# 128-row products in the scores and the compressed branch, and the softmax scaled on ScalarE with reciprocals taken a pack at a time

## The chip, the cores and the metric

One core of one Trainium2 chip runs the whole program. The metric is the device time of one execution in microseconds. TensorE (PE) does the matrix products and the transposes, VectorE (DVE) and ScalarE (ACT) the element-wise work, GpSimd (POOL) more of it, and SyncE (SP) issues every DMA. Each engine has its own queue of instructions.

## What is computed

Two decoder layers over 512 tokens of width 1024, in float32. One projection of the normed input feeds four groups of 4 heads x 64 wide: A (dilated windows), B (latent attention), C (compressed, selected and sliding-window attention, gated) and D (stick-breaking, no softmax). Each group's output is gated, then one output projection, a norm and the residual follow. Cut to what matters here:

```python
# A, B and the two block branches of C: per head and 128-query block
s = q @ k.T * scale                     # causal or dilated mask
p = exp(s - max(s)); p = p / sum(p)     # softmax
o = p @ v                               # C: times sigmoid(gate) per query
# C, compressed: 31 compressed keys/values of 64, all 4 heads
p_cmp = softmax(mask(q @ kc.T)); o_cmp = p_cmp @ vc
# D: z = q @ k.T * d**-0.5, then log-space products, a @ v
# layer: x + rms_norm(concat(o * silu(g)) @ w_out, g_post)
```

## The kernel before

Float32 operands are split into a high and a low part (type fp32r) and multiplied in three products, high x high, high x low and low x high; the fourth is dropped. All tiles of the two arenas (`arena_r` for split operands, `arena_f` for float32) are 512 columns wide. Of PSUM's eight banks, two hold scores, two hold transposes, one the outputs, and three take the projections.

The program is written as two generators per layer. `main` runs attention D, then B, C and A. `fill` runs the projections, gates and compressions, and last the output projection. `mix` (L1395 on) interleaves them by the ratios in `RATIO`. A scheduler then lays the instructions of each engine out in an order found by a model of the time at build, with the attention's instructions at raised priority. On the chip each engine runs its list in that order.

Attention goes by packs: one score bank of up to 512 columns holds one to four segments, and a segment is one head (in C one branch and head) and one query block `i`, 128*(i+1) columns wide. In one layer B has 10 packs, C 22 and A 11, together 64 segments; over both layers 86 packs and 128 segments. For A, C and D a score segment takes two products (`scores`, L973 and L974): stacked queries hold the high part in rows 0 to 63 and the low part in rows 64 to 127, the stacked keys hold the high part twice, so L973 does two of the three products with 128 rows, and L974 adds high query x low key with 64 rows. `scores_pair` (L983) does the same for two short segments of C. B keeps its own form (L964 to L966, 96 rows, three products).

`softmax` then goes segment by segment: a masked row extreme on DVE (L1016) gives the bias, ACT takes the exponential and its sum (L1018), DVE takes the reciprocal (L1019), in C multiplies it by the gate (L1022), and scales the segment (L1023). `turn` transposes 128x128 blocks on PE (L1100), splits them on ACT (L1103) and DVE (L1104), and `pv` multiplies with the values (L1116).

The compressed branch keeps its keys in one tile (`kcmp`, made at L936 to L940) and its scores in `cmp_soft` (L1066 with 128 rows, L1067 with 64, four heads). Its values (`vcmp`, L945 to L948) sit in rows 32h to 32h+31 for head h, and `pv` is called on 32 rows at a time.

Keys of A and C are put together by `key_stack` (DMAs within SBUF, all at L530), keys of D by `d_key` (L798 the high part, L801 the low part, one DMA for the copy of the high part). `split` makes the weights' high part on ACT or DVE (L307, L313, L315) and the low part on POOL (L308, L318) as weights come in (L282).

## Time and profile before

| | |
|---|---|
| median of three runs | 745.35 us (745.24 to 746.9) |
| profiled execution | 745.8 us, its span 744.0 us |
| TensorE clock granted, mean of the span | 0.959 |
| PE / DVE / ACT / POOL busy | 691.3 / 558.5 / 424.5 / 393.4 us |
| products and transposes on PE | 3464 |

Busy time is the union of an engine's instructions, and a product's end is modelled: consecutive products overlap in the records, so the time from one product's start to the next one's start tells what PE spends on it. Weight loads (PEld) stand on a row of their own and overlap the products. In the views below, a line that begins with a stretch such as 150.00:340.00 tells the busy time and the count of each engine in it; "idle ... <-" tells what ended an engine's idle time.

In time, layer 0 has D's scores from 56 to about 109 us, B from 150, C from 205 and A from 293 to 340 us; layer 1 has D from 410 to 466, B from 507, C from 563 and A from 650 to 700 us. Projections fill PE between and during these.

### The profile page before, as it was taken

Reading aid. Unit: us, or ns where it says so; the run is one execution under the profiler, and the core shown is the slowest. Engines: PE = TensorE matmul, PEld = TensorE weight load, DVE = VectorE, ACT = ScalarE, POOL = GpSimd, SP = SyncE. Lnnn points to the kernel's source line nnn. Section 1 sums busy time; section 2 is a strip of 40 time slices with the busy share of each in tenths; the row PEclk is TensorE's granted clock in tenths of the full one; section 3 lists DMA queues with packets and bytes.
Section 4 is the critical chain, followed back from the end, with each engine's and each line's share of the span. In section 5 each row is a group of like instructions: output and inputs, shape, how many; then the busy total and the mean of one; then the engine's idle time right before and its main releaser. Section 6 shows DMA issues by size and latency. Waiting matters only on the chain.

```text
span 744.0 us, 10331 instructions
## 1 busy us (share of the span) xinstructions
PE 691.3 (93%) x3464; PEld 544.7 (73%) x3464; DVE 558.5 (75%) x1150; ACT 424.5 (57%) x917; POOL 393.4 (53%) x299
## 2 busy tenths in 40 slices
PE   7998899399999999999979999979899998999996
PEld 6986677287866778768869787757786775877785
DVE  4937989879779698677693666987868889766833
ACT  5335676376467445785442666848745644566822
POOL 3828326665875242594581244286658526247710
PEclk9999899699998999999999999989999999899999
DMA  8437211634163024443442231047425204321041
GB/s 314 141 80 226 63 33 31 139 93 134 40 188 106 13 81 114 152 147 116 146 172 79 61 96 42 1 76 207 119 66 156 86 0 142 85 83 60 29 142 57
DMA packets 33733, 76.61 MB, mean 103 GB/s; under 512 B 6736, under 2 KB 15312, under 8 KB 33680
## 3 DMA queue, kind: packets, MB, share of 16 engines
q1 hardware_dynamic: 33680, 75.95, 33.8%
q8 instruction: 27, 0.44, 0.2%
q14 instruction: 26, 0.21, 0.1%
HBM read 57.71 MB, written 4.19 MB: 83 GB/s over the span
## 4 chain that ended last, share of the span: by engine, by line
PE 55%; DVE 27%; ACT 5%; issue 5%; SPq 3%; DMA 3%; POOL 2%; DVEq 0%; ACTq 0%; POOLq 0%
PE bank L454 8%; PE bank L455 7%; PE bank L457 6%; PE bank L446 5%; PE bank L444 5%; PE bank L445 5%; PE bank L1116 5%; PE bank L1100 4%; PE bank L974 4%; DVE arena_f L1052 3%; SPq L530 2%; PE bank L973 2%; DVE stats L1022 2%; DVE arena_f L1023 2%; DVE arena_f L873 2%
## 5 line engine op out<-in xcount | busy, mean ns | idle before, releaser
L318 POOL TENSOR_TENSOR arena_r<-raw,arena_r 128x512 fp32r<-128x512 f32 (+1 forms) x150 | 209.1, 1415 | 158.8 <-ACT arena_r L313 92.0
L454 PE MATMUL bank<-arena_r 128*128 128x512 f32 (+1 forms) x416 | 166.2, 404 | 21.2 <-DVE arena_r L780 17.8
L455 PE MATMUL bank<-arena_r 128*128 128x512 f32 (+1 forms) x416 | 163.7, 398 | 2.6 <-DVE arena_r L430 2.6
L454 PEld LDWEIGHTS bank<-arena_r 128*128 128x128 f32 x416 | 83.5, 201 | 39.8 <-DVE arena_r L780 18.5
L457 PE MATMUL bank<-arena_r 128*128 128x512 f32 (+1 forms) x416 | 108.8, 387 | 0.0
L444 PE MATMUL bank<-arena_r 128*128 128x256 f32 (+1 forms) x280 | 97.1, 347 | 1.5 <-ACT arena_r L429 1.4
L455 PEld LDWEIGHTS bank<-arena_r 128*128 128x128 f32 x416 | 83.7, 201 | 18.7 <-DVE arena_r L430 3.0
L445 PE MATMUL bank<-arena_r 128*128 128x256 f32 (+1 forms) x280 | 97.0, 346 | 0.0
L1018 ACT ACTIVATE arena_f<-arena_f,stats 128x384 f32<-128x384 f32 (+3 forms) x128 | 71.3, 559 | 43.9 <-DVE stats L1016 43.5
L446 PE MATMUL bank<-arena_r 128*128 128x256 f32 (+1 forms) x280 | 95.1, 346 | 0.0
L1104 DVE TENSOR_TENSOR arena_r<-bank,arena_r 128x512 fp32r<-128x512 f32 (+2 forms) x122 | 71.7, 597 | 30.7 <-ACT arena_r L1103 29.8
L1116 PE MATMUL bank<-arena_r 128*128 128x256 f32 (+5 forms) x368 | 84.0, 323 | 5.2 <-DVE arena_r L1104 4.2
L457 PEld LDWEIGHTS bank<-arena_r 128*128 128x128 f32 x416 | 73.7, 193 | 14.8 <-issue 2.1
L1103 ACT CAST arena_r<-bank 128x512 fp32r<-128x512 f32 (+2 forms) x122 | 61.1, 514 | 35.2 <-PE bank L1100 32.6
L1100 PE MATMUL bank<-consts,arena_f 128*128 128x128 f32 x408 | 74.8, 282 | 3.5 <-DVE arena_r L1104 3.4
L1016 DVE CUSTOM_DVE_ANT_0 arena_f<-bank,consts 128x512 f32<-128x512 f32 (+3 forms) x128 | 58.7, 483 | 20.9 <-PE bank L974 14.0
L1023 DVE TENSOR_SCALAR arena_f<-arena_f,stats 128x384 f32<-128x384 f32 (+3 forms) x128 | 72.9, 585 | 1.9
L308 POOL TENSOR_TENSOR arena_r<-raw,arena_r 128x512 fp32r<-128x512 f32 x34 | 47.7, 1414 | 46.3 <-ACT arena_r L307 37.1
L313 ACT CAST arena_r<-raw 128x1024 fp32r<-128x1024 f32 (+2 forms) x55 | 56.1, 1024 | 27.0 <-DMA raw<-w_in 10.9
L1116 PEld LDWEIGHTS bank<-arena_r 128*128 128x128 f32 (+2 forms) x368 | 51.7, 163 | 18.6 <-DVE arena_r L1104 5.3
L1100 PEld LDWEIGHTS bank<-consts,arena_f 128*128 128x128 f32 x408 | 52.2, 144 | 17.6 <-DVE arena_r L1104 5.1
L444 PEld LDWEIGHTS bank<-arena_r 128*128 128x128 f32 x280 | 53.9, 193 | 8.4 <-ACT arena_r L429 1.6
(163 smaller groups left out, 1226.4 us busy)
## 6 DMA issues: line engine op xcount, KB each, us to landing
raw<-w_in SPq DMA_DIRECT2D x56, 512.0 KB, 3.9
raw<-w_out SPq DMA_DIRECT2D x16, 512.0 KB, 3.3
arena_r<-arena_r SPq DMA_DIRECT2D x104, 64.0 KB, 2.0
arena_f<-x SPq DMA_DIRECT2D x8, 512.0 KB, 3.8
raw<-w1k SPq DMA_DIRECT2D x8, 512.0 KB, 3.8
arena_r<-arena_r SPq DMA_DIRECT2D x32, 128.0 KB, 2.5
raw<-w1v SPq DMA_DIRECT2D x8, 512.0 KB, 3.9
arena_f<-xs SPq DMA_DIRECT2D x4, 512.0 KB, 3.6
```

The lines of the kernel that those rows point to most:

```text
L318: nc.gpsimd.tensor_tensor(lo[:, q], raw[:, q], h[:, q].bitcast(F32), OP.subtract)
L444: mm(out, wh, xh, start=start, stop=False, skip_group_check=True)
L445: mm(out, wh, xl, start=False, stop=False, skip_group_check=True)
L446: mm(out, wl, xh, start=False, stop=stop, skip_group_check=True)
L454: mm(out[:, q], wh[:, k, :], self.h(0, k)[:, q], start=k == 0, stop=False, skip_group_check=True)
L455: mm(out[:, q], wh[:, k, :], self.h(1, k)[:, q], start=False, stop=False, skip_group_check=True)
L457: mm(out[:, q], wl[:, k - 8, :], self.h(0, k - 8)[:, q], start=False, stop=k == 15, skip_group_check=True)
L1018: nc.scalar.activation(x, x, AF.Exp, bias=nm, scale=-1.0, accum_out=l)
L1023: nc.vector.tensor_scalar(x, x, r, None, op0=OP.mult)
L1100: nc.tensor.transpose(t[:, 128 * j:128 * j + 128], b, self.ident)
L1104: nc.vector.tensor_tensor(lo[:, :w], t[:, :w], hi[:, :w].bitcast(F32), OP.subtract)
L1116: mm(o, v, x, start=first and n == 0, stop=last and n == 2 * len(jobs) - 1, skip_group_check=True)
```

## The change

Two parts.

Rows. Every low product of the scores (L974, L983, L1067) gets the full 128 rows. For that the low part of the keys is put twice into the stack, by wider DMAs in `key_stack` and by one more DMA in `d_key`; the product now also adds low x low. The compressed values go into a zeroed tile, head h in columns 128h to 128h+127 and rows 32h to 32h+31, so that `pv` can use all 128 rows for each head.

Softmax. The exponentials of a whole pack are taken first, then one reciprocal for the pack, then each segment is scaled by an ACT copy with the reciprocal as its scale. In C the gate is still multiplied in per segment on DVE.

```diff
@@ key_stack
-            self.dma(s[64 + 32 * j:96 + 32 * j, 0:512], p[:, 0:512])
+            self.dma(s[64 + 32 * j:96 + 32 * j], p)
@@ d_key, after the two subtractions of L801
+            self.dma(b[64:128], b[0:64])
@@ compress, keys
-            nc.vector.tensor_tensor(s[0:64, 352:384], o2[0:64, 0:32], s[0:64, 96:128].bitcast(F32), OP.subtract)
+            nc.vector.tensor_tensor(s[:, 352:384], o2[:, 0:32], s[:, 96:128].bitcast(F32), OP.subtract)
@@ compress, values
-            nc.scalar.copy(s[:, 0:64], o2[:, 0:64])
-            nc.vector.tensor_tensor(s[:, 64:128], o2[:, 0:64], s[:, 0:64].bitcast(F32), OP.subtract)
+            nc.vector.memset(s.ap.bitcast(F32), 0.0)
+            for h in range(4):
+                r, c = slice(32 * h, 32 * h + 32), 128 * h
+                nc.scalar.copy(s[r, c:c + 64], o2[r, 0:64])
+                nc.vector.tensor_tensor(s[r, c + 64:c + 128], o2[r, 0:64], s[r, c:c + 64].bitcast(F32), OP.subtract)
@@ scores
-        mm(out, qs[0:64, q], kb[0:64, :n], start=False, stop=True, skip_group_check=True)
+        mm(out, qs[:, q], kb[:, :n], start=False, stop=True, skip_group_check=True)
@@ scores_pair: x = k[0:r, ...] and Cq[h][0:r, ...] with r = 128, 64 become k[:, ...] and Cq[h][:, ...]
...
@@ softmax
-        a = 0
-        for br, h, i in segs:
+        a, k = 0, len(segs)
+        nm, l, r = self.col(k), self.col(k), self.col(k)
+        parts = []
+        for j, (br, h, i) in enumerate(segs):
             n = 128 * (i + 1)
             x, y = p[:, a:a + n], s[:, a:a + n]
             a += n
-            nm, l, r = self.col(), self.col(), self.col()
+            parts.append(x)
             nc.vector.tensor_tensor_reduce(out=x, in0=y, ..., accum_out=nm[:, j:j + 1])
-            nc.scalar.activation(x, x, AF.Exp, bias=nm, scale=-1.0, accum_out=l)
-            nc.vector.reciprocal(r, l)
+            nc.scalar.activation(x, x, AF.Exp, bias=nm[:, j:j + 1], scale=-1.0, accum_out=l[:, j:j + 1])
+        self.psfree(s)
+        nc.vector.reciprocal(r, l)
+        for j, (br, h, i) in enumerate(segs):
+            rj = r[:, j:j + 1]
             if m == "C":
                 g = 12 * i + 3 * h + 1 + br
-                nc.vector.tensor_tensor(r, r, self.gl[:, g:g + 1], OP.mult)
-            nc.vector.tensor_scalar(x, x, r, None, op0=OP.mult)
-        self.psfree(s)
+                nc.vector.tensor_scalar(rj, rj, self.gl[:, g:g + 1], None, op0=OP.mult)
+            nc.scalar.activation(parts[j], parts[j], AF.Copy, scale=rj)
@@ cmp_soft
-            nc.tensor.matmul(s, self.kcmp[0:64, 256 + a:384 + a], self.Cq[h][0:64], start=False, ...
+            nc.tensor.matmul(s, self.kcmp[:, 256 + a:384 + a], self.Cq[h].ap, start=False, ...
@@ attention, s3, compressed values
-                r = slice(32 * u[1], 32 * u[1] + 32)
-                self.pv([(o, (self.vcmp[r, 0:128], self.vcmp[r, 0:64]), [x[r] for x in pt])], False, last)
+                a = 128 * u[1]
+                self.pv([(o, (self.vcmp[:, a:a + 128], self.vcmp[:, a:a + 64]), [x.ap for x in pt])], False, last)
```

## Rows read from the trace of the kernel before

**Rows 1.** Page, section 1: busy us, share of the span, instructions.

```profile
PE 691.3 (93%) x3464; PEld 544.7 (73%) x3464; DVE 558.5 (75%) x1150; ACT 424.5 (57%) x917; POOL 393.4 (53%) x299
```

**Rows 2.** Timeline of PE: start us, us, engine, line, operation, rows*columns.

```profile
572.53 0.39 PE L455 MATMUL bank<-arena_r 128*128 128x512 f32 x1
572.75 0.39 PE L973 MATMUL bank<-arena_r 128*128 128x512 f32 x1
573.07 0.50 PE L974 MATMUL bank<-arena_r 64*128 64x512 f32 x1
573.50 0.50 PE L1066 MATMUL bank<-arena_r 128*128 128x512 f32 x1
573.92 0.50 PE L1067 MATMUL bank<-arena_r 64*128 64x512 f32 x1
```

**Rows 3.** Timeline of PE: short products between long ones.

```profile
659.33 0.32 PE L974 MATMUL bank<-arena_r 64*128 64x128 f32 x1
659.59 0.50 PE L454 MATMUL bank<-arena_r 128*128 128x512 f32 x1
659.92 0.22 PE L973 MATMUL bank<-arena_r 128*128 128x128 f32 x1
659.98 0.45 PE L455 MATMUL bank<-arena_r 128*128 128x512 f32 x1
```

**Rows 4.** Line L974: min/median/max ns, first and last start, forms.

```profile
L974 PE MATMUL bank<-arena_r x112: 276/436/792, 56.3 to 691.5; 64*128 64x384 f32 x32, 64*128 64x256 f32 x32, 64*128 64x512 f32 x32, 64*128 64x128 f32 x16
```

**Rows 5.** Waits: us in total, times, longest.

```profile
PEld bank L974 <- issue: 22.1, 86, 0.4
...
ACT arena_f L1018 <- DVE stats L1016: 43.5, 31, 6.6
```

**Rows 6.** Chain by line in 56:109, 205:293, 410:466, 563:650, 650:700, 507:534, in turn.

```profile
by line: DVE arena_f L1052 21.9%; DVE arena_f L1047 10.4%; issue 9.5%; DMA raw<-w_in 9.1%; DVE arena_f L1054 7.4%; DVE arena_f L1040 7.2%; PE bank L454 5.2%; PE bank L455 4.6%; PE bank L457 3.5%; PE bank L974 3.2%; PE bank L1100 2.8%; DVE a
...
by line: DVE arena_f L1023 10.1%; DVE stats L1022 10.0%; PE bank L454 8.0%; PE bank L455 7.5%; PE bank L1116 6.1%; PE bank L974 6.1%; PE bank L457 5.1%; DVE arena_f L1016 4.8%; PE bank L1100 4.7%; PE bank L973 4.0%; DVE arena_r L1104 3.7%; 
...
by line: PE bank L454 24.7%; PE bank L455 23.7%; PE bank L457 23.3%; PE bank L974 9.8%; PE bank L973 6.6%; PE bank L1116 4.1%; PE bank L1100 4.1%; PE bank L658 1.2%; PE bank L444 0.9%; PE bank L445 0.9%; PE bank L446 0.9%
...
by line: DVE stats L1022 9.7%; PE bank L454 9.2%; PE bank L455 8.9%; PE bank L974 8.4%; PE bank L457 7.8%; PE bank L1116 6.2%; PE bank L1100 6.2%; PE bank L973 5.7%; DVE arena_f L1023 5.1%; PE bank L906 4.4%; PE bank L445 3.4%; PE bank L444
...
by line: PE bank L1116 16.1%; PE bank L1100 9.0%; PE bank L455 8.8%; PE bank L974 8.6%; PE bank L454 8.5%; PE bank L444 8.4%; PE bank L445 8.4%; PE bank L446 8.1%; PE bank L457 7.8%; PE bank L973 5.0%; DVE arena_r L1104 3.0%; ACT arena_r L3
...
by line: DMA raw<-w1v 17.7%; ACT arena_r L313 14.4%; POOL arena_r L308 13.2%; ACT arena_f L1018 12.6%; POOL arena_r L318 11.3%; issue 11.0%; ACT arena_r L779 4.1%; PE bank L1116 3.4%; ACT arena_r L594 2.3%; ACT arena_f L1123 2.1%; ACT arena
```

**Rows 7.** Groups by line: busy us, mean ns, idle before.

```profile
L1018 ACT ACTIVATE arena_f<-arena_f,stats 128x384 f32<-128x384 f32 (+3 forms) x128 | 71.3, 559 | 43.9 <-DVE stats L1016 43.5
...
L1018 ACT ACTIVATE arena_f<-arena_f,stats 128x512 f32<-128x512 f32 x32 | 23.1, 723 | 18.1 <-DVE stats L1016 18.0
...
L1103 ACT CAST arena_r<-bank 128x512 fp32r<-128x512 f32 x74 | 42.5, 585 | 11.9 <-PE bank L1100 9.8 <-PE bank L455 0.8 <-PE bank L906 0.5
...
L1023 DVE TENSOR_SCALAR arena_f<-arena_f,stats 128x384 f32<-128x384 f32 (+3 forms) x128 | 72.9, 585 | 1.9
```

**Rows 8.** Line L1022: min/median/max ns.

```profile
L1022 DVE TENSOR_TENSOR stats<-stats,gl x64: 94/154/4935, 209.9 to 649.9; 128x1 f32<-128x1 f32 x64
```

**Rows 9.** Stretches: length, then busy us (count) by engine.

```profile
507.00:534.00 27.00, 26.08 (x138) 21.37 (x137) 24.48 (x76) 23.07 (x58) 20.88 (x16) 1.00 0.57 159
...
150.00:340.00 190.00, 185.29 (x940) 140.33 (x939) 153.47 (x411) 123.75 (x287) 116.28 (x90) 0.97 0.36 109
...
507.00:700.00 193.00, 184.86 (x915) 139.51 (x914) 154.21 (x409) 117.58 (x278) 112.67 (x89) 0.96 0.32 93
```

**Rows 10.** DMA issues: KB each, median us to landing.

```profile
arena_r<-arena_r SPq DMA_DIRECT2D x104, 64.0 KB, 2.0
...
arena_r<-arena_r SPq DMA_DIRECT2D x32, 128.0 KB, 2.5
```

**Rows 11.** Chain in order of time: start us, us, what.

```profile
54.07 4.83 DMA raw<-w_in
```

More of the change, by code (lines that the diff above doesn't have):

```diff
@@ L979, in scores_pair @@
         o = out.rearrange("p (b n) -> p b n", b=2)
-        for j, r in enumerate((128, 64)):
-            x = k[0:r, 512 * j:512 * j + 128]
+        for j in range(2):
+            x = k[:, 512 * j:512 * j + 128]
             x = bass.AP(tensor=x.tensor, offset=x.offset, ap=[x.ap[0], [d, 2], [1, 128]])
-            self.nc.tensor.matmul(o, self.Cq[h][0:r, 0:128], x, start=j == 0, stop=j == 1, skip_group_check=True)
+            self.nc.tensor.matmul(o, self.Cq[h][:, 0:128], x, start=j == 0, stop=j == 1, skip_group_check=True)
     def val(self, m, br, h, kb):
@@ L1014, in softmax @@
             a += n
-            nm, l, r = self.col(), self.col(), self.col()
+            parts.append(x)
             nc.vector.tensor_tensor_reduce(out=x, in0=y, in1=self.c[:, base + 512 - n:base + 512], scale=-sc,
-                                           scalar=3e38, op0=OP.add, op1=OP.min, accum_out=nm)
-            nc.scalar.activation(x, x, AF.Exp, bias=nm, scale=-1.0, accum_out=l)
-            nc.vector.reciprocal(r, l)
+                                           scalar=3e38, op0=OP.add, op1=OP.min, accum_out=nm[:, j:j + 1])
+            nc.scalar.activation(x, x, AF.Exp, bias=nm[:, j:j + 1], scale=-1.0, accum_out=l[:, j:j + 1])
[3 more added lines that the diff above has]
+            rj = r[:, j:j + 1]
             if m == "C":
                 g = 12 * i + 3 * h + 1 + br
-                nc.vector.tensor_tensor(r, r, self.gl[:, g:g + 1], OP.mult)
-            nc.vector.tensor_scalar(x, x, r, None, op0=OP.mult)
-        self.psfree(s)
+                nc.vector.tensor_scalar(rj, rj, self.gl[:, g:g + 1], None, op0=OP.mult)
+            nc.scalar.activation(parts[j], parts[j], AF.Copy, scale=rj)
         return p
@@ L1066, in cmp_soft @@
             nc.tensor.matmul(s, self.kcmp[:, a:a + 128], self.Cq[h].ap, start=h == 0, stop=False, skip_group_check=True)
-            nc.tensor.matmul(s, self.kcmp[0:64, 256 + a:384 + a], self.Cq[h][0:64], start=False, stop=h == 3,
+            nc.tensor.matmul(s, self.kcmp[:, 256 + a:384 + a], self.Cq[h].ap, start=False, stop=h == 3,
                              skip_group_check=True)
```

## The prediction, made before the changed kernel ran

> **What bounds the kernel now.** The page's first section comes first: PE is busy 93% of the span, DVE 75%, ACT 57% [rows 1]. A busy PE may still be a slow PE, so I went to the timeline of PE and read starts, not durations. In a dense run a 512-column product starts 0.22 to 0.23 us after the one before it (572.53 to 572.75). Around products of 64 rows the pace breaks: L973 to L974 0.32 us, L974 to L1066 0.43, L1066 to L1067 0.42 [rows 2]. With 128 columns it is plainer: after L974 the next product starts 0.26 us later (659.33 to 659.59), after the equally short 128-row L973 0.06 us later (659.92 to 659.98) [rows 3]. So each change between 128 and 64 rows costs PE up to 0.20 us beyond the columns, on the way in and on the way out. The waits say the same from the other side: PEld sits idle 22.1 us in 86 places before L974 while the profile shows nothing that it waits for [rows 5].
>
> Then the chain of waits by stretch [rows 6]. It runs over PE lines in D of layer 1 (410:466) and in A (650:700), over PE and DVE in C (L1022, L1023), mostly over DVE in D of layer 0 (56:109). The stretch 507:534, B of layer 1, runs over ACT, POOL and a load. So PE's lost time is mostly on the path that sets the end, but not everywhere.
>
> **Part by part: the rows.** L974 runs 112 times, of 128, 256, 384 and 512 columns (16, 32, 32, 32), 347 on average [rows 4]; from the code L983 and L1067 add 8 each with 64 rows, 128 in all. The columns stay the same; only the breaks go. Per 64-row product the break is 0.32 + 0.43 - 2 x 0.23 = 0.29 us at the low end and 2 x 0.20 = 0.40 at the high end [rows 2, 3]; I take 0.35, the middle, since both kinds are frequent. That is 128 x 0.35 = 45 us of PE time (37 to 51). The 16 products of `pv` with 32 rows have no row here; by the nearest they gain 0 to 0.20 each, 0 to 3 us, taken as 1.
>
> How much of it lies on the path? I take L973 and L974 from the chain's shares [rows 6]: C of layer 0 10.1% of 88 us = 8.9; D of layer 1 16.4% of 56 = 9.2; C of layer 1 14.1% of 87 = 12.3; A of layer 1 13.6% of 50 = 6.8; A of layer 0, which has the same code, by the same share of 47 us = 6.4; D of layer 0 3.2% of 53 = 1.7. Sum 45.3 us. An average pair takes 2 x 0.23 x 347/512 = 0.31 us of columns and 0.35 of breaks, so 53% of its time is breaks: 24 us. L983 and L1067 hold 16 x 0.35 = 5.6 us, of which I count 4, as they stand in C where PE leads the chain only in part, and the 32-row products 1. Sum: 29 us off the path.
>
> What it adds. `key_stack` moves 24 transfers from 64 to 128 KB, 2.0 to 2.5 us from issue to landing [rows 10]; scores come long after for most of them: 0 to 2 us, taken 0.5. `d_key` issues four more DMAs on SP. Behind the first of them are the weight loads, and the one at 54.07 us is on the chain with 4.83 us [rows 11]; an issue is part of the 2.0 us from issue to landing [rows 10], so 0 to 2 us, taken 0.5. The low product of D's first pack now also waits for a copy (2.5 us or more [rows 10]) that starts after the subtraction: 0 to 3 us per layer, taken 0, because projections fill PE there. The two more tile clears, six more short casts and six more subtractions of `vcmp` are charged nothing, since the compressed product comes last in its pair of heads; uncovered they cost at most 3.5 us.
>
> **Part by part: the softmax.** DVE sheds 128 scalings, 72.9 us [rows 7], and 42 of 128 reciprocals. ACT gains 128 copies. The trace has no copy with a scale from a column; the nearest is the exponential of the same sizes with a bias from a column, 0.559 us on average, 71.6 us in all. The other end is a plain cast: 0.585 against 0.723 at 512 columns, so 0.81 x 71.6 = 58 us [rows 7]. I take the first, which has the same operands.
>
> A scaling on DVE takes 0.585 us on average [rows 7] and on ACT by this 0.559, so on the chain of C (L1023: 10.1% of 88 and 5.1% of 87 us [rows 6]) the exchange brings nothing by itself. L1022, the gate's product, stays on DVE 64 times; its median is 0.154 us and its longest 4.9 [rows 8], and ACT's copies of that pack, and all that is queued on ACT behind them, now wait for it: the casts of transposed blocks (L1103), of weights (L313) and the copies of outputs (L1123), and PE waits for those. I take nothing for it in the sum; a rival holds it.
>
> Is there room on ACT? From 150 to 340 us ACT works 123.75 us, from 507 to 700 us 117.58 [rows 9]. B, C and A of one layer add 64 x 0.559 = 35.8: 159.5 and 153.4 us. The densest stretch in which the chain goes over ACT is 507:534, at 23.07/27 = 85% [rows 6, 9]. At that density the two regions need 187 and 180 us, against 190 and 193 now: 3 + 13 = 16 us come off, and with D's share (5.6 us in layer 1, 1.5 in layer 0) 23. With the cheap copies (29 us a layer) they need 179 and 172, and 11 + 17 + 7 = 35 come off, the 17 being PE's own limit there (48 products x 0.35). So ACT allows 23 to 35 us, and the chain's 29 stands in the middle.
>
> **The sum.** 745.8 - 29 + 0.5 + 0.5 = 717.8 us for the profiled execution, whose span is 744.0; the median of the runs is 0.45 lower, which gives 717.4.
>
> **The rivals.** (1) PE gives back all: ACT has room and every break was on the path. 45 + 1 us come off: 700. For it: PE's 93%. Against: the stretches of D in layer 0 and of B, where DVE and ACT lead.
>
> (2) ACT becomes the bound of B, C and A, with waits on top. ACT's exponentials wait for DVE 43.5 us now, over 128 of them 0.34 us each [rows 5]; if each of the 86 packs adds one such wait for its reciprocal, 29 us, and half of it isn't covered, the gain falls from 29 to 14: 732. The Trainium skill, ScalarE: Activation LUTs, Rules for kernel authors, speaks for it: it says to use VectorE, not ScalarE, for mul. In this trace DVE's scaling is no cheaper than ACT's estimate, so by the duration alone the rule doesn't decide.
>
> (3) Slower: ACT's queue stands still at the copies. When an exponential does wait for DVE, it waits 43.5/31 = 1.4 us [rows 5]. If every one of 86 packs does so, ACT needs 312.9 + 120 = 433 us for regions of 383: 50 us more, less D's 7, 789 us. The point from which it decides: (383 + 7 - 312.9)/86 = 0.9 us a pack. Against: only 31 of 128 exponentials wait at present, and ACT has other work to stand between.
>
> (4) The rows bring nothing: the breaks belong to the place of these products, not to their 64 rows. Then only the softmax part acts: in 507:534 ACT takes 16 x 0.559 = 8.9 us more on the chain, 745.8 + 9 = 755. Against: the same place, one product later, shows 0.06 us with 128 rows and 0.26 with 64 [rows 3]. The Trainium skill, TensorE: Matmul & The Clock Gate, Why this matters for your kernels, would put its weight here: it says that a single product with K=32 takes the same time as one with K=128. By that rule no row edit helps; the trace differs from it by those 0.20 us.
>
> **Chances and range.** Forecast, 708 to 728: 0.50. Rival 1, 693 to 708: 0.14. Rival 2, 728 to 743: 0.20. Rival 3, above 748: 0.09. Rival 4: 0.03. Within 0.3%, where rival 2 goes somewhat further: 0.04. 0.3% is about what a measurement of this kernel can tell from no change. So faster 0.84, same 0.04, slower 0.12. The range 698 to 740 leaves out rivals 3 and 4 and thin ends of 1 and 2, and takes in the bounds of the breaks and of the copies.
>
> **What would show it.** After the change, L974 and L1067 start 0.22 to 0.23 us after a 512-column product and the next as soon after them; idle time by "issue" before L974 goes from 22.1 to a few us; the sum of PE's busy time falls below 660. ACT's busy time is 482 to 496 us, and the line of the new copies has about 0.56 us each. DVE falls to some 480 us. If rival 2 or 3 holds, the waits show ACT's copies waiting for DVE's reciprocal or for L1022's successor with more than 29 us in total, and the chain in B and A goes over ACT. I am wrong in the first step if the breaks stay with 128 rows, in the second if the chain moves to ACT or DVE by as much as PE gains.

## The result, and the profile after

The changed kernel takes 717.78 us (715.55 to 718.75), 0.9629 of the kernel before [0.9594, 0.9664]; the prediction was 717.4. Its profiled execution took 718.75 us, with a span of 716.9.

The page of the changed kernel: busy us, share of the span and instructions; the engines' shares of the chain; then three groups (busy us, mean ns | idle before, releaser).

```profile
PE 650.3 (91%) x3464; PEld 540.1 (75%) x3464; DVE 482.4 (67%) x988; ACT 477.7 (67%) x1051; POOL 391.7 (55%) x299
...
PE 41%; DVE 25%; ACT 16%; issue 6%; DMA 4%; POOL 4%; SPq 3%; DVEq 0%; ACTq 0%; POOLq 0%
...
L1112 DVE TENSOR_TENSOR arena_r<-bank,arena_r 128x512 fp32r<-128x512 f32 (+2 forms) x122 | 71.8, 597 | 57.6 <-ACT arena_r L1111 55.5
...
L1024 ACT ACTIVATE arena_f<-arena_f,stats 128x512 f32<-128x512 f32 (+3 forms) x128 | 71.1, 558 | 9.1 <-DVE stats L1022 8.5
...
L1032 ACT ACTIVATE arena_f<-arena_f,stats 128x512 f32<-128x512 f32 (+3 forms) x128 | 66.1, 557 | 3.8 <-DVE stats L1031 3.0
```

Against [rows 1], PE lost 41.0 us and DVE 76.1, and ACT gained 53.2. L1032 is the new copy on ACT, 0.557 us each. L1024 is the exponential, L1018 of before: its waits for DVE fell from 43.5 us [rows 5] to 8.5. DVE has time to spare instead, and waits 55.5 us for ACT's casts in L1112. Line numbers have moved: L977 and L978 are the two products of `scores` (L973 and L974 before), L1074 and L1075 those of the compressed branch (L1066 and L1067), L1111 and L1112 ACT's cast and DVE's subtraction on a transposed block (L1103 and L1104).

The timeline of PE in the changed kernel at two places (start us, us, engine, line), which answer to [rows 2] and [rows 3]:

```profile
559.02 0.40 PE L977 MATMUL bank<-arena_r 128*128 128x512 f32 x1
559.26 0.40 PE L978 MATMUL bank<-arena_r 128*128 128x512 f32 x1
559.50 0.40 PE L1074 MATMUL bank<-arena_r 128*128 128x512 f32 x1
559.74 0.40 PE L1075 MATMUL bank<-arena_r 128*128 128x512 f32 x1
...
629.90 0.22 PE L978 MATMUL bank<-arena_r 128*128 128x128 f32 x1
629.96 0.45 PE L454 MATMUL bank<-arena_r 128*128 128x512 f32 x1
```

Both the low product and the one after it now start 0.24 us after the one before, instead of 0.32 to 0.43; behind a low product of 128 columns the next one starts 0.06 us later, instead of 0.26. The idle time by "issue" before the low product, 22.1 us [rows 5], is gone as well: L978 waits 1.3 us in all, for transfers. So the breaks are gone. TensorE's mean granted clock is 0.957 here and was 0.959, so it is not the clock that makes the changed kernel faster.

To see where the time went, I cut the span at the first and the last exponential of each layer: B begins with the one and A ends with the other, and D lies ahead of each. The line of the exponential by layer (ns min/median/max, first and last start), of before:

```profile
L1018 ACT ACTIVATE arena_f<-arena_f,stats x64: 385/561/732, 156.1 to 339.0; 128x128 f32<-128x128 f32 x16, 128x384 f32<-128x384 f32 x16, 128x256 f32<-128x256 f32 x16, 128x512 f32<-128x512 f32 x16
...
L1018 ACT ACTIVATE arena_f<-arena_f,stats x64: 387/557/727, 512.2 to 698.7; 128x128 f32<-128x128 f32 x16, 128x384 f32<-128x384 f32 x16, 128x512 f32<-128x512 f32 x16, 128x256 f32<-128x256 f32 x16
```

and of the changed kernel:

```profile
L1024 ACT ACTIVATE arena_f<-arena_f,stats x64: 393/568/735, 165.1 to 330.5; 128x128 f32<-128x128 f32 x16, 128x384 f32<-128x384 f32 x16, 128x256 f32<-128x256 f32 x16, 128x512 f32<-128x512 f32 x16
...
L1024 ACT ACTIVATE arena_f<-arena_f,stats x64: 386/560/727, 502.7 to 671.5; 128x128 f32<-128x128 f32 x16, 128x384 f32<-128x384 f32 x16, 128x512 f32<-128x512 f32 x16, 128x256 f32<-128x256 f32 x16
```

The differences are +9.0 us up to the first exponential, -17.5 from B to A of layer 0, -1.0 between the layers, -17.7 from B to A of layer 1 and +0.1 behind: -27.1 in all. The two stretches with D in them lose 8 us where a gain was forecast, and the two stretches from B to A gain far more than forecast. The experiments follow these two surprises. All runs, with the same five stretches of their profiled executions in us:

| kernel | time, us | ratio to before | start | layer 0, B to A | between | layer 1, B to A | rest |
|---|---|---|---|---|---|---|---|
| before, in the runs beside these | 745.3 to 747.1 | 1 | 156.1 | 182.9 | 173.2 | 186.5 | 45.3 |
| the change | 717.78 | 0.9629 [0.9594, 0.9664] | 165.1 | 165.4 | 172.2 | 168.8 | 45.4 |
| rows_only | 733.32 | 0.9814 [0.9788, 0.9841] | 164.5 | 180.4 | 170.7 | 171.9 | 44.4 |
| soft_only | 742.07 | 0.9943 [0.9923, 0.9963] | 155.5 | 182.5 | 173.4 | 182.1 | 45.4 |
| both64 | 739.49 | one run | 157.4 | 179.8 | 168.6 | 185.1 | 46.8 |
| rows_c_act | 718.27 | 0.9612 [0.9587, 0.9636] | 164.2 | 175.8 | 171.3 | 161.3 | 45.1 |
| rows_pack_dve | 724.17 | 0.9733 [0.9674, 0.9791] | 163.1 | 168.8 | 178.2 | 167.2 | 44.5 |
| rows_gate | 718.44 | 0.9630 [0.9594, 0.9665] | 164.0 | 167.6 | 170.3 | 170.7 | 44.8 |
| after_tt | 718.55 | 0.9627 [0.9604, 0.9649] | 163.5 | 166.3 | 169.9 | 172.2 | 45.9 |
| d_rows_only | 741.64 | 0.9948 [0.9925, 0.9970] | 163.7 | 183.9 | 172.4 | 174.4 | 45.8 |
| rows_no_d | 713.94 | 0.9579 [0.9530, 0.9627] | 157.6 | 170.5 | 172.8 | 166.5 | 44.7 |
| d_act | 712.65 | 0.9555 [0.9510, 0.9599] | 154.1 | 173.7 | 169.2 | 169.3 | 45.2 |
| d_act_2 | 712.75 | 0.9533 [0.9506, 0.9561] | 154.3 | 173.1 | 169.0 | 169.4 | 45.1 |
| d_act_c | 713.20 | 0.9557 [0.9532, 0.9582] | 155.6 | 171.1 | 176.1 | 161.6 | 45.9 |

Projections fill PE in all stretches and move from one to another, so a difference of a few us in one stretch alone says little. The start is the firm one: every kernel in which D's low keys are copied by a transfer begins B at 163 to 165 us, every other at 154 to 158.

### The profile page after: what moved, and what is told of

Its sections match the earlier page's. It is cut to its first block, busy times and chain, and to the rows that moved or that the text cites. A ratio compares the mean times of both kernels' runs of the same rounds, so it can differ in the third digit from the quotient of the medians.

```text
span 716.9 us, 10366 instructions
## 1 busy us (share of the span) xinstructions
PE 650.3 (91%) x3464; PEld 540.1 (75%) x3464; DVE 482.4 (67%) x988; ACT 477.7 (67%) x1051; POOL 391.7 (55%) x299
## 4 chain that ended last, share of the span: by engine, by line
PE 41%; DVE 25%; ACT 16%; issue 6%; DMA 4%; POOL 4%; SPq 3%; DVEq 0%; ACTq 0%; POOLq 0%
PE bank L454 5%; PE bank L455 5%; PE bank L446 5%; PE bank L444 5%; PE bank L445 5%; PE bank L1124 4%; PE bank L457 4%; DVE arena_f L1060 3%; PE bank L1108 3%; ACT arena_f L1024 3%; SPq L530 3%; ACT arena_f L1032 2%; DVE arena_f L874 2%; DMA raw<-w_in 2%; POOL arena_r L318 2%
## 5 line engine op out<-in xcount | busy, mean ns | idle before, releaser
L454 PE MATMUL bank<-arena_r 128*128 128x512 f32 (+1 forms) x416 | 162.6, 395 | 10.9 <-DVE arena_r L780 5.0
L455 PE MATMUL bank<-arena_r 128*128 128x512 f32 (+1 forms) x416 | 160.5, 391 | 2.4 <-DVE arena_r L430 2.4
L1112 DVE TENSOR_TENSOR arena_r<-bank,arena_r 128x512 fp32r<-128x512 f32 (+2 forms) x122 | 71.8, 597 | 57.6 <-ACT arena_r L1111 55.5
L457 PE MATMUL bank<-arena_r 128*128 128x512 f32 (+1 forms) x416 | 104.9, 379 | 0.0
L454 PEld LDWEIGHTS bank<-arena_r 128*128 128x128 f32 x416 | 82.3, 198 | 27.9 <-DVE arena_r L780 5.2
L1124 PE MATMUL bank<-arena_r 128*128 128x256 f32 (+4 forms) x368 | 88.4, 332 | 13.7 <-ACT arena_r L1111 6.6
L455 PEld LDWEIGHTS bank<-arena_r 128*128 128x128 f32 x416 | 82.3, 198 | 16.2 <-DVE arena_r L430 2.9
L457 PEld LDWEIGHTS bank<-arena_r 128*128 128x128 f32 x416 | 73.3, 190 | 12.7
L1124 PEld LDWEIGHTS bank<-arena_r 128*128 128x128 f32 (+1 forms) x368 | 55.5, 170 | 28.9 <-ACT arena_r L1111 9.3
L1024 ACT ACTIVATE arena_f<-arena_f,stats 128x512 f32<-128x512 f32 (+3 forms) x128 | 71.1, 558 | 9.1 <-DVE stats L1022 8.5
L1108 PE MATMUL bank<-consts,arena_f 128*128 128x128 f32 x408 | 73.3, 280 | 1.1 <-DVE arena_r L1112 0.7
L1111 ACT CAST arena_r<-bank 128x512 fp32r<-128x512 f32 (+2 forms) x122 | 60.9, 513 | 18.0 <-PE bank L1108 11.7
L1022 DVE CUSTOM_DVE_ANT_0 arena_f<-bank,consts 128x512 f32<-128x512 f32 (+3 forms) x128 | 58.3, 484 | 20.2 <-PE bank L978 10.1
L1032 ACT ACTIVATE arena_f<-arena_f,stats 128x512 f32<-128x512 f32 (+3 forms) x128 | 66.1, 557 | 3.8 <-DVE stats L1031 3.0
L444 PEld LDWEIGHTS bank<-arena_r 128*128 128x128 f32 x280 | 53.6, 192 | 18.9 <-ACT arena_f L1063 11.7
L1108 PEld LDWEIGHTS bank<-consts,arena_f 128*128 128x128 f32 x408 | 53.2, 144 | 12.5 <-DVE arena_r L1112 1.8
```

Source lines behind the costliest of these rows:

```text
L444: mm(out, wh, xh, start=start, stop=False, skip_group_check=True)
L454: mm(out[:, q], wh[:, k, :], self.h(0, k)[:, q], start=k == 0, stop=False, skip_group_check=True)
L455: mm(out[:, q], wh[:, k, :], self.h(1, k)[:, q], start=False, stop=False, skip_group_check=True)
L457: mm(out[:, q], wl[:, k - 8, :], self.h(0, k - 8)[:, q], start=False, stop=k == 15, skip_group_check=True)
L1024: nc.scalar.activation(x, x, AF.Exp, bias=nm[:, j:j + 1], scale=-1.0, accum_out=l[:, j:j + 1])
L1032: nc.scalar.activation(parts[j], parts[j], AF.Copy, scale=rj)
```

## The experiments

**The two halves of the change, each alone.** `rows_only` takes the changed kernel and gives it the softmax of before; `soft_only` takes the kernel before and gives it the changed softmax.

```
rows_only, against the changed kernel, in the softmax:
-        nc.vector.reciprocal(r, l)
-        for j, (br, h, i) in enumerate(segs):
...
-                nc.vector.tensor_scalar(rj, rj, self.gl[:, g:g + 1], None, op0=OP.mult)
-            nc.scalar.activation(parts[j], parts[j], AF.Copy, scale=rj)
+            nc.vector.reciprocal(r, l)
...
+                nc.vector.tensor_tensor(r, r, self.gl[:, g:g + 1], OP.mult)
+            nc.vector.tensor_scalar(x, x, r, None, op0=OP.mult)
```

> Only the row part of the change: every product of scores, pairs and the compressed branch with 128 rows; the softmax stays segment by segment with DVE's scaling, as before. My theory (the forecast's sum, which gave the softmax nothing): the rows carry the whole gain, 716 to 721 us, and PEld's idle time by issue before the low product falls from 22.1 us to under 4. Rival (DVE's relief is part of the gain): the rows alone give less than two thirds of it, 726 to 734 us, and DVE leads the chain in C. Second rival (the softmax part costs ACT's time and the rows paid for it): under 713 us.

> Only the softmax part: reciprocals by pack and the scaling on ACT; the low products keep 64 rows as before. My theory: nothing in C (0.585 us on DVE against 0.559 on ACT) and up to 9 us more in B of layer 1, where ACT leads the chain: 744 to 755 us. Rival (DVE's relief counts): 730 to 740 us. Rival 3 of the forecast (ACT's queue stands still at the copies) would give over 760 us.

Measured, from the ratios and 745.3 us: 13.9 us for the rows and 4.2 for the softmax; 18.1 as a sum, 27.7 together. Neither the forecast's split, all for the rows and nothing for the softmax, nor a plain sum holds; 742.07 lies below the 744 to 755 that I expected of `soft_only`. The page of `rows_only` (busy time, chain), and from B to A of layer 0 its chain by line and a window (length, then busy us and count of PE, PEld, DVE, ACT and POOL, clock, DMA share, GB/s), and one of its waits:

```profile
PE 655.0 (89%) x3464; PEld 542.3 (74%) x3464; DVE 571.0 (78%) x1158; ACT 421.9 (58%) x923; POOL 393.8 (54%) x299
...
DVE 41%; PE 40%; ACT 8%; issue 5%; POOL 2%; DMA 2%; SPq 1%; DVEq 0%; ACTq 0%; POOLq 0%
...
by line: DVE arena_f L1027 16.7%; DVE arena_f L1020 5.9%; DVE stats L1026 5.8%; DVE arena_r L1108 5.5%; PE bank L1120 5.1%; PE bank L1104 4.2%; PE bank L454 4.0%; issue 3.8%; PE bank L455 3.6%; PE bank L446 2.7%; PE bank L444 2.3%; PE bank 
...
155.00:346.00 191.00, 172.32 (x920) 141.80 (x919) 162.75 (x414) 120.72 (x286) 110.27 (x86) 0.94 0.37 110
...
ACT arena_f L1022 <- DVE stats L1020: 67.2, 40, 5.8
```

PE gave back its breaks here too (655.0 us). But DVE, 81% busy in this stretch before [rows 9], is now 85%, and the chain stands on its scaling (L1027), its masked minimum (L1020) and its gate's product (L1026). ACT's exponentials wait 67.2 us for DVE, where it was 43.5 [rows 5]. So with the rows alone the chain of layer 0 goes over DVE, and relief for DVE is what the softmax part is worth; how little relief is enough is tried below. In the changed kernel the two stretches read (same columns):

```profile
155.00:332.00 177.00, 167.90 (x923) 140.07 (x922) 115.12 (x329) 148.45 (x350) 111.02 (x86) 0.95 0.40 119
497.00:673.00 176.00, 164.94 (x913) 134.49 (x912) 115.53 (x328) 143.78 (x346) 108.30 (x87) 0.99 0.37 110
```

DVE is at 65 and 66%, ACT at 84 and 82%.

**Is it the change of rows, or the 64 rows?** `both64` leaves the kernel before as it is, but for the first product of `scores`, which also reads 64 rows; the product of the queries' low part with the keys' high part is left out by that.

```
-        mm(out, qs[:, q], ka[:, :n], start=True, stop=False, skip_group_check=True)
+        mm(out, qs[0:64, q], ka[0:64, :n], start=True, stop=False, skip_group_check=True)
```

> The kernel before, with the first score product (A, C, D) cut to 64 rows too, so that low query x high key is left out of the scores. Theory (the change between 128 and 64 rows costs up to 0.20 us each way, the rows themselves nothing): the low product starts 0.23 us after a 512-column first one, not 0.32 to 0.43, each pair still pays on its way in and out, and the time is 735 to 748 us. Rival (a 64-row product is slow in itself): 112 more slow ones, 39 us more of PE, low product 0.43 us after the first, 765 to 785 us.

Measured: 739.5 us. The rival's 765 to 785 us did not come, and 64 rows behind 64 rows do not take its 0.43 us. But a row of 64-row products isn't free of breaks either. Timeline of PE and two waits (us in total, times, longest) of `both64`, and, last, two of B's products, which have 96 rows, in the kernel before:

```profile
671.50 0.49 PE L973 MATMUL bank<-arena_r 64*128 64x512 f32 x1
671.83 0.39 PE L974 MATMUL bank<-arena_r 64*128 64x512 f32 x1
672.15 0.73 PE L446 MATMUL bank<-arena_r 128*128 128x512 f32 x2
...
PEld bank L973 <- issue: 11.0, 40, 0.4
...
PEld bank L974 <- issue: 4.3, 19, 0.3
...
512.16 0.40 PE L964 MATMUL bank<-arena_r 96*128 96x512 f32 x1
512.39 0.40 PE L965 MATMUL bank<-arena_r 96*128 96x512 f32 x1
```

From 64 to 64 rows it is 0.33 us (671.50 to 671.83), and out to 128 rows 0.32: 0.10 too much each. Before, the way out cost 0.20 [rows 2, 3]. The idle time before the low product fell from 22.1 us [rows 5] to 4.3, and 11.0 came before the first one. So each border that a 64-row product touches costs 0.10 to 0.20 us, one between two of them too. And fewer than 128 rows need not break the pace at all: B's products of 96 rows start 0.23 us after one another. No run tried 96 rows for the low products.

**Which relief does DVE need?** Three kernels vary the softmax with all rows at 128. `rows_c_act` lets ACT scale only in C, and DVE in A and B. `rows_pack_dve` leaves all scalings on DVE, with the reciprocals a pack at a time.

```
rows_c_act, against the changed kernel:
-            nc.scalar.activation(parts[j], parts[j], AF.Copy, scale=rj)
+            if m == "C":
+                nc.scalar.activation(parts[j], parts[j], AF.Copy, scale=rj)
+            else:
+                nc.vector.tensor_scalar(parts[j], parts[j], rj, None, op0=OP.mult)
rows_pack_dve, against the changed kernel:
-            nc.scalar.activation(parts[j], parts[j], AF.Copy, scale=rj)
+            nc.vector.tensor_scalar(parts[j], parts[j], rj, None, op0=OP.mult)
```

> The changed kernel with the scaling on ACT in C alone; in B and A (64 of 128 segments) DVE scales, reciprocals still by pack. ACT sheds 64 x 0.557 = 36 us. Theory (ACT leads B and has no room in A): faster than the changed kernel by 3 to 8 us, 709 to 715. Rival (PE leads in A and projections cover B): within 3 us of 717.8. Second rival (DVE's share of B and A was worth something): 720 to 725 us.

> All rows, reciprocals by pack, but every scaling on DVE. Rows alone took 733 us, the whole change 718. Theory (DVE is the bound of C in layer 0 once PE is quicker, so its 70 us of scalings are what counts): 728 to 735 us. Rival (the order by packs and the fewer reciprocals are what counts): 716 to 722 us.

`rows_c_act` is as fast as the change, not 3 to 8 us faster as I expected: which engine scales in A and B makes no difference that can be measured. `rows_pack_dve` is 9 us faster than `rows_only` by the medians (6 by the ratios, whose intervals just touch), though DVE does all its scalings; 724 lies between the two ranges that I expected. What the two share and `rows_only` lacks, beside the reciprocals by pack, is a small edit inside the change that the prediction had passed over: in C, the product of the reciprocal with the gate, a 128x1 operation, is a tensor_scalar and no longer a tensor_tensor. So I tried that edit alone, and its reverse:

```
rows_gate, against rows_only:
-                nc.vector.tensor_tensor(r, r, self.gl[:, g:g + 1], OP.mult)
+                nc.vector.tensor_scalar(r, r, self.gl[:, g:g + 1], None, op0=OP.mult)
after_tt, against the changed kernel:
-                nc.vector.tensor_scalar(rj, rj, self.gl[:, g:g + 1], None, op0=OP.mult)
+                nc.vector.tensor_tensor(rj, rj, self.gl[:, g:g + 1], OP.mult)
```

> Rows alone (733 us) with one thing of the softmax part: C's gate product as a tensor_scalar with the gate as a column, not as a tensor_tensor of two columns. In the traces that line takes 0.443 us on average as a tensor_tensor (27 us, longest 4.9 us) and 0.206 as a tensor_scalar (11 us). Theory (the gate's form is most of what the order by packs gave, 733 to 724 us): 723 to 728 us. Rival (the packs' order and the 42 fewer reciprocals gave it): 731 to 735 us.

> The changed kernel with C's gate product as a tensor_tensor again, all else as changed. Theory (that form waits for POOL, 16 us over 64 of them, and ACT's copies now wait behind it): 722 to 730 us, and its mean goes back above 0.4 us. Rival (with DVE relieved of the scalings these waits are covered): 716 to 720 us.

`rows_gate` reaches the whole gain of the change, 718.44 us, more than I expected (723 to 728), with all 128 scalings and reciprocals on DVE as before. `after_tt` came out as its rival had it, 718.55. The gate's line (ns min/median/max) in `rows_only`:

```profile
L1026 DVE TENSOR_TENSOR stats<-stats,gl x64: 127/158/3734, 220.6 to 642.3; 128x1 f32<-128x1 f32 x64
```

in `rows_gate`, with its window from B to A of layer 0, and one of its products beside an operation of POOL:

```profile
L1026 DVE TENSOR_SCALAR stats<-stats,gl x64: 107/202/218, 218.5 to 628.6; 128x1 f32<-128x1 f32 x64
...
154.00:335.00 181.00, 169.46 (x938) 139.52 (x937) 154.83 (x414) 121.24 (x286) 111.75 (x86) 0.98 0.39 117
...
588.54 0.21 DVE L1026 TENSOR_SCALAR stats<-stats,gl 128x1 f32<-128x1 f32 x1
588.28 1.48 POOL L544 TENSOR_TENSOR arena_f<-arena_f,tab 128x512 f32<-128x512 f32 x1 [12.35 <-ACT arena_f L538]
```

in `after_tt`:

```profile
L1031 DVE TENSOR_TENSOR stats<-stats,gl x64: 140/159/4732, 213.7 to 623.5; 128x1 f32<-128x1 f32 x64
```

and the longest one of `rows_only`, with POOL beside it:

```profile
569.91 3.73 DVE L1026 TENSOR_TENSOR stats<-stats,gl 128x1 f32<-128x1 f32 x1
569.79 1.34 POOL L566 TENSOR_TENSOR arena_f<-arena_f 128x512 f32<-128x512 f32 x1
571.09 2.53 POOL L318 TENSOR_TENSOR arena_r<-raw,arena_r 128x512 fp32r<-128x512 f32 x2
```

The tensor_scalar has the longer median (0.202 against 0.158 us), but none of 64 is longer than 0.218, where the tensor_tensor reaches 3.7 and 4.7. By the groups, that is 27.5 against 12.2 us of DVE in all, in C, where the chain went over this line before too [rows 6, 8]. What the long ones wait for is POOL: this one started 0.12 us after a POOL operation with two inputs and ended at 573.64, 0.02 us after the third of three such operations in a row. In the traces of the kernel before, of `rows_only` and of `after_tt` all 52 products above 0.3 us end 0.01 to 0.10 us after such an operation of POOL. As a tensor_scalar, 26 of the 64 in `rows_gate` lie wholly inside one, and none is held. In `after_tt` the long ones are back (25.7 us), and the time stays: with the scalings off DVE there is room to hide them. So DVE needs one relief or the other, and both together bring no more than one.

Where the gate's edit gains is another matter. Of the 14.5 us between the spans of `rows_only` and `rows_gate`, 12.8 lie from B to A of layer 0, and there the gate's products give back 8.6 us of DVE (14.69 to 6.07). In A, where no such product runs, `rows_only` has the longest operation of DVE in all these profiles, and it stands on the chain (DVE's timeline, then the chain in order of time):

```profile
310.38 8.44 DVE L1027 TENSOR_SCALAR arena_f<-arena_f,stats 128x384 f32<-128x384 f32 x1
...
310.38 8.44 DVE arena_f L1027
```

It is one scaling of 384 columns, where the median scaling takes 0.44; it ended 0.2 us after the last of eight POOL operations that followed one another. In `rows_gate` no scaling takes more than 3.0. So up to 8 us of the gate's gain, and of what `rows_only` lacks against the change, are this one wait. The edit does not touch that scaling; why the wait is gone with it is open. No second profile of `rows_only` tells whether the wait is there each time; its six runs lie at 728.9 to 735.9, all above every run of `rows_gate` (716.9 to 721.8). That `rows_pack_dve` stands 6 us above `rows_gate` stays open (its three runs spread over 5 us); by the table its loss lies between the layers (178.2 against 170.3 us), not from B to A.

**D's rows and their transfer.** `rows_no_d` is the change without D: its low product keeps 64 rows, and the transfer in `d_key` is not issued. `d_rows_only` is the kernel before with D's part alone. `d_act` is the change with the copy of D's low keys on ACT.

```
rows_no_d, against the changed kernel:
-            self.dma(b[64:128], b[0:64])
...
-        mm(out, qs[:, q], kb[:, :n], start=False, stop=True, skip_group_check=True)
+        r = 64 if m == "D" else 128
+        mm(out, qs[0:r, q], kb[0:r, :n], start=False, stop=True, skip_group_check=True)
d_rows_only, against the kernel before, beside the transfer:
+        r = 128 if m == "D" else 64
d_act, against the changed kernel:
-            self.dma(b[64:128], b[0:64])
+            nc.scalar.copy(b[64:128], b[0:64].bitcast(F32))
```

> The changed kernel, but D's low product keeps 64 rows and d_key its single DMA. The trace of the changed kernel shows D of layer 0 starting some 2 us later and lasting 51 us against 50, and D of layer 1 lasting 56 against 54, with the chain on DVE. Theory now (DVE leads D as soon as PE doesn't, so D's rows bring nothing and its DMA costs a little): 711 to 717 us. Rival (the forecast: D's breaks are on the path, 6.6 us): 722 to 726 us.

> The kernel before, with D's low product alone on 128 rows and the copy of D's low keys. Theory now: D doesn't end earlier, 745 to 751 us. Rival (the forecast's term for D, 1.5 + 5.6 us): 737 to 741 us.

> The changed kernel with the copy of D's low keys made by one ACT copy instead of a DMA on SP. Theory (the DMA on SP ahead of the weight loads and the wait for its landing delay D of layer 0 by up to 2 us): 714 to 717 us, D of layer 0 starts 1 to 2 us earlier. Rival (the DMA is covered; D's length is DVE's): within 1.5 us of the changed kernel.

Without D's part the change is 3.8 us faster (713.94), with intervals that overlap a little; with the copy on ACT it is 5.1 faster (712.65, and 712.75 the second time). So the transfer costs about 5 us, and D's rows, once they cost no transfer, bring 1.3 us or nothing: the intervals of `rows_no_d` and `d_act` overlap. `d_rows_only` gains 3.9 us in spite of the transfer, between the range that I expected (no gain) and its rival, from B to A of layer 1 (174.4 for 186.5) and not in D. So D's part helps the kernel before and, by those 3.8 us, rather hurts the changed one; which work it lets ahead in the one and not in the other isn't settled.

How four transfers between buffers come to cost 5 us is seen first at the start of D in layer 0. SP's queue in the changed kernel (start us, us), with one of its waits over the whole run:

```profile
53.70 1.18 SPq L530 DMA_DIRECT2D arena_r<-arena_r  x2
54.97 2.75 SPq L282 DMA_DIRECT2D raw<-w_in  x4
...
SPq L530 <- DVE arena_r L801: 5.7, 3, 3.2
```

and before:

```profile
52.85 0.54 SPq L530 DMA_DIRECT2D arena_r<-arena_r  x1
53.49 2.16 SPq L282 DMA_DIRECT2D raw<-w_in  x4
```

The weight loads start 1.5 us later, of which the new issue makes 0.6 and the rest is not its own: the first copy starts 0.85 later too, behind 22 transfers to `tab` where it stood behind 21; ACT's longest wait for a load grows from 6.5 to 8.0 us. The new transfer holds the queue in a second way: SP stands still 5.7 us in three places until DVE has made the low part (L801), with loads behind it; `d_act` has no such transfer. And POOL's subtractions of these weights move against DVE's scans of D. The scans in the changed kernel (all sizes, then 128 columns), with the timelines of POOL and of DVE at one place in layer 1:

```profile
L1060 DVE TENSOR_TENSOR_SCAN arena_f<-arena_f,consts 128x128 f32<-128x128 f32 (+3 forms) x32 | 39.5, 1268 | 0.2
...
L1060 DVE TENSOR_TENSOR_SCAN arena_f<-arena_f,consts 128x128 f32<-128x128 f32 x8 | 8.5, 1062 | 0.0
...
411.11 2.94 POOL L318 TENSOR_TENSOR arena_r<-raw,arena_r 128x512 fp32r<-128x512 f32 x2 [8.29 <-ACT arena_r L313]
...
411.48 3.12 DVE L1060 TENSOR_TENSOR_SCAN arena_f<-arena_f,consts 128x256 f32<-128x256 f32 x2
```

before:

```profile
L1052 DVE TENSOR_TENSOR_SCAN arena_f<-arena_f,consts 128x128 f32<-128x128 f32 (+3 forms) x32 | 32.7, 1053 | 0.2
...
L1052 DVE TENSOR_TENSOR_SCAN arena_f<-arena_f,consts 128x128 f32<-128x128 f32 x8 | 4.4, 554 | 0.1
```

and in `d_act`:

```profile
L1060 DVE TENSOR_TENSOR_SCAN arena_f<-arena_f,consts 128x128 f32<-128x128 f32 (+3 forms) x32 | 33.9, 1087 | 0.2
...
L1060 DVE TENSOR_TENSOR_SCAN arena_f<-arena_f,consts 128x128 f32<-128x128 f32 x8 | 3.8, 477 | 0.1
```

The same 32 scans take 39.5 us in the changed kernel and 38.7 to 39.6 in every kernel with the transfer, `d_rows_only` too; without it 28.0 to 34.8. A scan beside POOL's subtraction takes over twice its time: 1.56 us for 256 columns at 411.48, against a mean of 0.675 in that layer before. Against `d_act` the scans take 5.6 us more, about half of it in each layer. DVE leads the chain in D of layer 0 [rows 6] and, in the changed kernel, in D of layer 1 too. So longer scans, a later start and SP's waits are together of the right size for the 5.1; how the loss divides between them was not tried.

**Both best parts, and a second run.** `d_act_c` has the copy of D's keys on ACT and ACT's scaling in C alone. `d_act_2` is `d_act` again, beside it.

> The changed kernel with D's low keys copied by ACT, and the scaling on ACT in C alone (DVE scales in B and A). Theory (B and A don't care which engine scales, as C alone on ACT took the same time as all on ACT): 710 to 715 us. Rival (ACT's copy of D's keys gains only where ACT has room, so both gains add to under 710): 704 to 710 us.

> The changed kernel with D's low keys copied by ACT once more, beside the kernel with C alone on ACT on the same chip. Theory: 711 to 715 us, 3 to 6 us under the changed kernel, as before. Rival (the first look was a lucky order): 716 to 719 us.

713.20 and 712.75 us: no difference, so giving ACT less brings nothing here either. `d_act` is the best version, at 0.9555 and 0.9533 of the kernel before, 5 us below the change.

## Why the prediction was right, and where it wasn't

**The breaks: right, in size and kind.** 45 + 1 us of PE were forecast (37 to 51), 41.0 were measured, and the low product now starts at the pace of the others. The rival that the place and not the rows makes the breaks, at 755, is refuted: the same place lost them with 128 rows. The rule weighed there, from the Trainium skill, TensorE: Matmul & The Clock Gate, Why this matters for your kernels, that a single product with K=32 takes the time of one with K=128, does not carry over to this kernel's products of 64 rows among others: they lose 0.10 to 0.20 us at each border. `both64` and B's 96 rows show that my reading, each change between 128 and 64 rows costs, was too narrow: two products of 64 rows break the pace as well, and 96 rows don't.

**The share on the path: the total right, the parts not.** Forecast were 29 us off, by their terms 23.2 from B to A (10.6 in layer 0 and 12.6 in layer 1) and 5.8 in D, less 1 for the transfers. Measured were 35.2 from B to A and 8.0 lost in the two stretches that hold D. Part of that is a mere shift of projections between the stretches, but `rows_no_d` and `d_act` tell the terms within their intervals, 2 to 4 us to either side: D's was 5.8 and is 0 to 1.3, the one from B to A was 23.2 and is some 31, what the change brings without D (`rows_no_d`, 4.21% of 745.3). (The check of ACT's room in the prediction counted D with 7.1 us, 5.6 and 1.5, where the sum has 5.8; neither came.)

The step that failed for D is the one that multiplied L974's share of the chain [rows 6] by the part of its time that was breaks. In D of layer 1 the chain ran over PE almost alone, but beneath it DVE was not far behind. Chain by line in 413:467 of the kernel before, with its window:

```profile
by line: PE bank L454 24.8%; PE bank L457 24.1%; PE bank L455 24.1%; PE bank L974 9.6%; PE bank L973 6.1%; PE bank L1116 4.3%; PE bank L1100 4.2%; ACT arena_f L663 1.3%; PE bank L658 1.3%; ACT arena_r L520 0.9%; issue 0.0%
...
413.00:467.00 54.00, 54.00 (x238) 41.17 (x238) 39.26 (x63) 35.12 (x60) 20.89 (x15) 1.00 0.21 60
```

and in 400:457 of the changed kernel, with its window:

```profile
by line: DVE arena_f L1060 23.2%; issue 9.7%; DVE arena_f L1055 7.8%; DVE arena_f L1062 7.5%; DVE arena_f L1048 7.4%; PE bank L454 5.3%; PE bank L455 4.7%; DVE arena_r L1112 4.0%; ACT arena_f L1053 3.0%; DVE arena_f L1134 2.4%; POOL arena_f
...
400.00:457.00 57.00, 50.98 (x242) 41.32 (x241) 45.37 (x64) 36.72 (x65) 21.04 (x15) 0.97 0.24 67
```

The stage is no shorter, PE has 6 us of gaps in it where it had none, DVE's busy time grew from 39.26 to 45.37 us with the longer scans, and the chain went over to them.

**The transfer in `d_key`: mis-sized.** Forecast 0.5 us (0 to 2), it cost about 5. The issue's length (0.54 us) and the late load (1.5 us) were the right rows; that SP's queue would wait 5.7 us for DVE's subtraction with the loads behind it, and that later loads move POOL's work onto DVE's scans, were not in the sum. The wait of D's low product for it, taken as 0 (0 to 3 a layer), is right: before L978 PE is idle 1.3 us for transfers in the whole run.

**The softmax: duration right, worth wrong.** The copy was taken at 0.559 us and has 0.557; ACT's busy time rose to 477.7, 4 under the lower end of 482; DVE's 482.4 is the forecast 480. "The exchange brings nothing by itself" is what failed. It compared two means, though DVE's scalings have a median of 0.421 us and a longest of 1.55 before (L1023) and ACT's copies 0.560 and 0.745 (L1032), and left out that with PE's breaks gone the chain would go over DVE, so that relief for DVE counts: the softmax part is worth 4.2 us without the rows and 13.8 with them (27.7 less 13.9). The Trainium skill, ScalarE: Activation LUTs, Rules for kernel authors, sends such a product to VectorE; against `rows_gate`, which follows it, the change is neither faster nor slower.

**L1022, the gate's product: the step that was read wrongly.** The prediction let it stay on DVE with its long waits. The change replaces it by a tensor_scalar, which never waits long, and with the rows at 128 this edit alone is worth 14 to 15 us (`rows_only` 733.32 to `rows_gate` 718.44; 13.7 by the ratios), up to 8 of them through the one scaling that waits for POOL in `rows_only`. The row that says so was there: median 0.154, longest 4.9 us [rows 8], and 10% of the chain in C [rows 6].

**The rivals with ACT.** Neither 732 nor 789 came: the copies wait 3.0 us for DVE's products and 0.5 for its reciprocals in total, where more than 29 us was the rivals' sign, and the exponentials wait 8.5. ACT's density was the right thing to ask, at 84 and 82% from B to A. It can go higher than the 85% I took as its limit; the changed kernel at the start of B of layer 1, chain by line and window:

```profile
by line: ACT arena_f L1024 28.5%; ACT arena_r L313 14.9%; ACT arena_f L1032 11.7%; ACT arena_r L779 8.6%; ACT arena_r L594 6.6%; ACT arena_r L307 5.5%; ACT arena_f L573 3.4%; ACT arena_f L1131 3.1%; ACT arena_f L916 3.0%; ACT arena_f L574 2
...
497.00:516.00 19.00, 17.78 (x97) 13.91 (x96) 14.24 (x49) 18.31 (x45) 10.71 (x9) 1.00 0.71 201
```

ACT works 96% of it and leads the chain there, as forecast for B.

So 717.4 came out at 717.78 in part by luck: some 8 us too little were forecast for the rows from B to A with the relief of DVE, 4 to 5 too much for D, and 4 to 5 too little for the price of the transfer. Behind it stands a larger one: by the sum, the rows alone would have come to 717, and they came to 733. The other half of the gain came with the relief of DVE, or with the end of the 8.4 us wait, and the sum had neither.

## What to carry to other kernels

Take an engine's lost time off the path only down to where the next engine stands: read the second engine's density and its long waits in the same stretch. Two edits, one on each engine, can bring more together than the sum of both alone (here 27.7 us against 18.1); but look first for a single long wait in the run with one edit, which may be most of the difference, as the 8.4 us here. A median of 0.15 us beside a maximum of 5 in a tiny operation marks a wait that another form of the instruction may not have; try that form first, as it did as much here as moving 73 us of work to another engine. Before a transfer is put ahead of loads, ask what it waits for in the queue, what the later loads move, and on whom that falls.

## What the runs showed of the hardware that I had not expected

- Two consecutive products of 64 rows lose 0.10 us as well (0.33 us from start to start at 512 columns, against 0.23 with 128 rows); products of 96 rows do not (0.23).
- DVE's 128x1 product as a tensor_tensor takes 0.16 us, but up to 4.9 beside POOL; as a tensor_scalar with the factor from a column, 0.2 us and never above 0.22. The Trainium skill, SBUF — State Buffer, SBUF: two separate sides, has a rule that fits: DVE's operations with two inputs in SBUF share a port with GpSimd's operations that read SBUF, and the one that comes first holds it for its whole instruction. The traces bear it out: the long ones end 0.01 to 0.10 us after an operation of POOL, and one can wait for several in a row (three for the 3.73 us above). A tensor_scalar of whole segments is not free of such waits: DVE's scaling, 0.44 us by its median in `rows_only`, took up to 8.4 there beside POOL.
- DVE's scan of 256 columns takes 0.675 us on average in D of layer 1 before, and two beside POOL's subtractions took 3.12 us.
